# Hybrid decoder layer: an earlier copy of q's sums, other PSUM banks for the woven projections, a larger wait weight

## The chip, the cores and the metric

One core of one Trainium2 chip. The metric is the device time of one execution in microseconds (us). The kernel before takes 595.57 us, the median of three runs (594.65 to 597.58).

## The reference

One decoder layer over 16 meta tokens and 1024 positions, width 1024, everything in float32. An RMS norm is followed by one input projection. Its columns feed two groups of heads that read the same normalised input; the outputs go through one output projection, a residual and a last RMS norm.

```python
u = rmsnorm(h, norm_g)                                  # h: 1040 x 1024
q, k, v, f, z_attn, gate_b, gate_c, xc, z_conv = split(u @ w_in)
cum = cumsum(log_sigmoid(f + b_f))                      # per head
s = q @ k.T / 8 + cum[t] - cum[s]                       # causal, 8 heads x 64
attn = softmax(s) @ v
y_attn = group_rmsnorm(attn, attn_norm_g, 8) * silu(z_attn)
conv = causal_conv3(gate_c * xc, conv_w)                # 512 channels
y_conv = group_rmsnorm(gate_b * conv, conv_norm_g, 8) * silu(z_conv)
out = rmsnorm(h + concat(y_attn, y_conv) @ w_out, final_norm_g)[16:]
```

## The kernel before, in words

Every float32 product is made of three matmuls: each operand is split into a rounded part (`xhi`, `wmhi`, made on ScalarE or GpSimd) and a remainder (`xlo`, `wmlo`, made on VectorE by `lo_vec`, line 115), and hi x hi, hi x lo and lo x hi add up in one PSUM bank.

**First stage, q (lines 179 to 250).** The eight PSUM banks hold the eight sums of q (`psq[m][c]`, four blocks of 128 columns by two halves of the positions): seven tiles of the pool `ps1` and one of `psx`. While inputs arrive, each of eight row slabs adds to all eight banks. After them ScalarE copies the four sums with c = 0 (line 240) and VectorE those with c = 1 (line 241) to SBUF. Ahead of the input projections' scaling stands the row norm: nine loads of `h` through SyncE's queue (line 249), each squared and summed on ScalarE (line 250); `rsqrt_small` (lines 78 to 89) makes the factors, TensorE transposes them into a bank of `psx` (line 259) and VectorE copies them (line 260).

**k, v and the gates (lines 263 to 384).** k's blocks go through the seven `ps1` banks in turn; the first k block takes the bank that q's sum (0, 0) held. Each chunk is scaled by VectorE (`kf`, line 275) and split; q, k and v go to DRAM. The last three chunks of k block 3 take the `ps1` banks 6, 0 and 1, and the `psx` bank last held the transposed decay sums (lines 374 to 377).

**The woven stage (lines 387 to 765).** Here the eight banks are dealt out anew: `pj` (two banks, for the projections), `psn` (three, scores), `pst` (two, transposes), `pso` (one, the products with v). Sixteen half heads of attention are the main work: scores and their exponentials (`s_step`), the end of a softmax (`s_end`: the maximum on VectorE, some small operations on GpSimd, ScalarE and VectorE, then GpSimd scales the exponentials in place, line 635), transposes (`t_step`) and products with v (`v_step`). The twenty projections of the convolution and the gates, in 384 steps of three matmuls, are the filler. `weave` (lines 745 to 760) deals them out: each main step has a cost in us, and after it so many filler steps follow that the rest of the filler is spread evenly over the rest of the main cost; `HEAD` us of filler go ahead of the first scores, `LEFT` us stay. The end of a softmax costs `WAIT`, which stands for no matmul: it draws filler between the scores and the transposes that need the scaled values. `WAIT` has one value for half heads of the one kind, one for the other, and a third for the very first softmax. The filler goes in the order gate c, x, convolution gate, attention gate, gate b for each of four column blocks; with the last step of an x block (line 458) comes a convolution: a scaling pass on GpSimd (line 460) and three passes on VectorE (lines 461 to 463).

TensorE keeps this written order for everything from the first woven projection on. The order of the other engines' instructions, and that of SyncE's DMAs apart from those that are kept in program order, is set by a planner at build time; it may differ from the order of the code.

**Output (lines 769 to 861).** Six of the banks are dealt out again, weights and gated outputs are split as they arrive, and the output projection, residual and last norm follow.

Of the kernel before, what the change touches and what calls it, by code (L numbers as in the profile page):

```python
# [11 lines left out]
AF = mybir.ActivationFunctionType  # L12
ALU = mybir.AluOpType
AX = mybir.AxisListType
PSUM = bass.MemoryType.PSUM
# [20 lines left out]
def hybrid_kernel(ctx, tc, hT, h, w_q, w_vf, w_m, w_o, gn, bf, cw, ga, gc, gf, out):  # L36
    nc = tc.nc
    R_SIDE = "right"
    TABLES = "natural_log_exp_and_others"

    def f(ap):
        return ap.bitcast(F32)
# [49 lines left out]
    def behind(ins):  # L92

        tc.keep_in_program_order(ins)
# [5 lines left out]
    def after(ins, name):  # L100

        tc.add_manual_dep(ins.ins, name, mybir.DependencyInfo(
            mybir.DependencyClass.NoSync, mybir.DependencyReason.SCHED_ONLY), reason="pace")
# [10 lines left out]
    def lo_vec(lo, src, hi):  # L114
        nc.vector.tensor_tensor(lo, src, f(hi), ALU.subtract)  # L115
# [15 lines left out]
    def load_w(m):  # L131
        staged[m] = wp.tile([P, KT, P], F32, name="wm", bufs=1)
        ins = nc.sync.dma_start(staged[m], w_m[m].rearrange("p (k c) -> p k c", k=KT))
        if m < 4:
            behind(ins)

    def split_w(m):
        ws = staged.pop(m)
        whi = wp.tile([P, KT, P], F32R, name="wmhi")
        wlo = wp.tile([P, KT, P], F32R, name="wmlo")  # L140
        hi_pool(whi, ws)
        lo_vec(wlo, ws, whi)
        ready[m] = whi, wlo
# [35 lines left out]
    with ExitStack() as ca:  # L179
# [23 lines left out]
        for i in range(8):  # L203
# [3 lines left out]
        psq = [[(psx if (m, c) == (3, 1) else ps1).tile([P, 512], F32, name="px" if (m, c) == (3, 1) else "ps")  # L207
                for c in range(2)] for m in range(4)]
        with ExitStack() as c1:
            wq = c1.enter_context(tc.tile_pool(name="wq", bufs=3))  # L210
            for k in range(KT):
                ws = wq.tile([P, 512], F32, name="ws")
                xs = wq.tile([P, L], F32, name="xs")
                whi = wq.tile([P, 512], F32R, name="wqhi")
                wlo = wq.tile([P, 512], F32R, name="wqlo")
                if k == 0:
                    behind(nc.sync.dma_start(xs[:, :528], hT[:, 0, :528]))
                behind(nc.sync.dma_start(ws, w_q[k * P:(k + 1) * P, :]))
                (nc.vector.tensor_copy if k == 0 else nc.scalar.copy)(whi, ws)
                for a, b in ((0, 528), (528, L)) if k == 0 else ((0, L),):  # L220
                    if a or k:
                        behind(nc.sync.dma_start(xs[:, a:b], hT[:, k, a:b]))
                    nc.scalar.activation(xhi[k][:, a:b], xs[:, a:b], AF.Copy, scale=gnt[:, k:k + 1])
                    nc.vector.scalar_tensor_tensor(xlo[k][:, a:b], xs[:, a:b], gnt[:, k:k + 1], f(xhi[k][:, a:b]),
                                                   ALU.mult, ALU.subtract)
                lo_vec(wlo, ws, whi)
                todo = [(m, n, c) for m in range(4) for n in range(3) for c in range(2)]
                if k == 0:
                    todo.sort(key=lambda t: t[1:])
                for m, n, c in todo:  # L230
                    wt, xt = ((whi, xhi[k]), (whi, xlo[k]), (wlo, xhi[k]))[n]
                    nc.tensor.matmul(psq[m][c], wt[:, m * P:(m + 1) * P], xt[:, NM + 512 * c:NM + 512 * c + 512],
                                     start=(k == 0 and n == 0), stop=(k == KT - 1 and n == 2))
            load_w(0)
            split_w(0)
            for t, v in ((bft, bf.broadcast_to([P, HEADS])), (cwt, cw), (gat, ga), (gct, gc)):
                behind(nc.sync.dma_start(t, v))
            qraw = [[qk.tile([P, 512], F32, name=f"qraw{m}{c}") for c in range(2)] for m in range(4)]
            for m in range(4):
                nc.scalar.copy(qraw[m][0], psq[m][0])  # L240
                nc.vector.tensor_copy(qraw[m][1], psq[m][1])


            ss = sm.tile([P, 9], F32, name="ss")
            nc.vector.memset(ss, 1.0)
            for j in range(9):
                n = P if j < 8 else NM
                ht = st.tile([P, D], F32, name="ht")
                behind(nc.sync.dma_start(ht[:n], h[j * P:j * P + n, :]))
                nc.scalar.activation(ht[:n], ht[:n], AF.Square, accum_out=ss[:n, j:j + 1])  # L250
        nc.vector.tensor_scalar(ss, ss, 1.0 / D, EPS, ALU.mult, ALU.add)
        rsqrt_small(sm, ss, rtok, "x")
        for b in range(3):
            pr = psx.tile([P, 512], F32, name="px")
            w = 512 if b < 2 else NM
            for i in range(4 if b < 2 else 1):
                j = 4 * b + i
                n = P if j < 8 else NM
# [57 lines left out]
        for j in (0, 1, 2, 3, 5, 6, 7, 4, 8):  # L316
            n = P if j < 8 else NM
# [68 lines left out]

    own = ctx.enter_context(tc.tile_pool(name="own", bufs=1, reuse_waits="tile"))
    cp = ExitStack()
    pj = ctx.enter_context(tc.tile_pool(name="pj", bufs=2, space=PSUM, reuse_waits="tile"))
    psn = cp.enter_context(tc.tile_pool(name="psn", bufs=3, space=PSUM, reuse_waits="tile"))  # L390
    pst = cp.enter_context(tc.tile_pool(name="pst", bufs=2, space=PSUM, reuse_waits="tile"))
    pso = cp.enter_context(tc.tile_pool(name="pso", bufs=1, space=PSUM, reuse_waits="tile"))
# [165 lines left out]
    T_AT = (0.065, 0.08)  # L558
    V_END = 0.975
    V_LAG = 3  # L560
    WAIT = (0, 0.375, 3.3)
    SOON = 0.2
    HEAD = 15.75
    LEFT = 2.75
# [51 lines left out]
    def s_end(c):  # L616

        mx = pnp.tile([P, 4], F32, name="mx")
        nc.vector.tensor_reduce(mx, nmx[c], AX.X, ALU.min)
        e = pnp.tile([P, 4, 3], F32, name="e")  # L620
        nc.gpsimd.tensor_tensor(e, mx.unsqueeze(2).broadcast_to([P, 4, 3]), nmx[c], ALU.subtract)
        nc.scalar.activation(e, e, AF.Exp)
        t = pnp.tile([P, 4, 3], F32, name="t")
        nc.gpsimd.tensor_mul(t, e, smx[c])
        s = pnp.tile([P, 4], F32, name="s")
        nc.gpsimd.tensor_add(s, t[:, :, 0], t[:, :, 1])
        nc.gpsimd.tensor_add(s, s, t[:, :, 2])
        nc.vector.reciprocal(s, s)
        fc = pnp.tile([P, 4, 3], F32, name="fc", bufs=2)
        nc.gpsimd.tensor_mul(fc, e, s.unsqueeze(2).broadcast_to([P, 4, 3]))  # L630
        for i in range(3):
            for j in range(4 * c, 4 * c + 4):
                if i < len(SCH[j]):
                    k0, w = SCH[j][i]
                    nc.gpsimd.tensor_scalar(pn[j][:, k0:k0 + w], pn[j][:, k0:k0 + w], fc[:, j % 4, i:i + 1], 1.0,  # L635
                                            ALU.mult, ALU.mult)
# [70 lines left out]
    def spread(steps, todo, lo, hi):  # L707

        whole = sum(x for x, _ in todo) or 1.0
        at = 0.0  # L710
        for x, s in todo:
            steps.append((lo + (hi - lo) * (at + x / 2) / whole, x, s))
            at += x

    stages = []
    for g in range(-1, 2 * HEADS):
# [3 lines left out]
        if g + 1 < 2 * HEADS:  # L720
# [4 lines left out]
            spread(steps, todo, lo, hi)  # L725
            steps.append((hi, WAIT[g % 2 if g >= 0 else 2], lambda c=c: s_end(c)))
        if g >= 0:
# [55 lines left out]
    def out_mm(n, es):  # L783
        t, c0, w = cells[n]
        tt, cs = slice(t * P, t * P + P), slice(c0, c0 + w)
        for e in es:
            for i, (a, b) in enumerate(((mhi[e], whi[e]), (mhi[e], wlo[e]), (mlo[e], whi[e]))):
                ins = nc.tensor.matmul(held[n][:, :w], a[:, tt], b[:, cs], start=(e == ORDER[0] and i == 0),  # L788
                                       stop=(e == ORDER[-1] and i == 2))
                if n < AHEAD:  # L790
                    pinned(ins)
        return ins.ins.name
# [42 lines left out]
    for i, e in enumerate(ORDER):  # L835
# [7 lines left out]
        for k, n in enumerate(ring):  # L843
            name = out_mm(n, [e])
# [63 lines left out]
```

## Time and profile before

| what | value |
|---|---|
| median of three runs | 595.57 us (594.65 to 597.58) |
| the profiled execution | 596.83 us |
| its span, first to last instruction | 595.1 us |
| TensorE busy, mean granted clock | 578.0 us (97%), 0.995 of full speed |
| VectorE busy | 377.9 us (64%) |
| ScalarE busy | 285.4 us (48%) |
| GpSimd busy | 168.0 us (28%) |

PE is TensorE's matmuls, DVE VectorE, ACT ScalarE, POOL GpSimd, SP the queue of DMA issues on SyncE. Times in the timeline are microseconds from the start of the span. "out<-in" names the tiles that an instruction writes and reads. A bracket at the end of a row is idle time of that engine just before it and what ended it.

### The profile page before, as it was taken

How to read it: one execution, taken by the hardware profiler on the slowest of the kernel's cores; microseconds unless marked ns; L12 is line 12 of the kernel's file. 1: busy time of each engine (PE TensorE's matmuls, PEld its weight loads, DVE VectorE, ACT ScalarE, POOL GpSimd, SP SyncE). 2: the span in 40 equal slices, each digit the busy share in tenths (PEclk: the TensorE clock that was granted, in tenths of full speed). 3: DMA queues.
4: the chain of work that ended last, by engine and by line, in shares of the span. 5: the costliest groups of instructions: out<-in, count | busy, mean ns of one | idle time of the engine just before them, and what ended most of it. 6: DMA issues, size and time to landing. Idle time of an engine off the chain costs nothing.

```text
span 595.1 us, 9156 instructions
## 1 busy us (share of the span) xinstructions
PE 578.0 (97%) x3230; PEld 509.6 (86%) x3230; DVE 377.9 (64%) x834; ACT 285.4 (48%) x667; POOL 168.0 (28%) x290
## 2 busy tenths in 40 slices
PE   9999999999998999999999999999999999899995
PEld 6888999999997889988879997889998887688884
DVE  5415851133367686879776888868869777947432
ACT  5355431131044575556764655747636676705221
POOL 1002010121027244151243254430552416710000
PEclk9999999999999999999999999999999999899999
DMA  8764594249811605415126134251350227453201
GB/s 287 237 194 141 195 341 142 70 147 280 262 39 36 144 35 135 120 57 155 44 75 143 71 108 112 75 143 37 111 197 16 73 88 243 171 205 113 100 35 70
DMA packets 35221, 78.14 MB, mean 131 GB/s; under 512 B 4024, under 2 KB 13384, under 8 KB 35176
## 3 DMA queue, kind: packets, MB, share of 16 engines
q1 hardware_dynamic: 35032, 77.57, 41.6%
q8 instruction: 25, 0.41, 0.3%
q14 instruction: 20, 0.16, 0.1%
q10 hardware_dynamic: 144, 0.00, 0.0%
HBM read 55.92 MB, written 21.64 MB: 130 GB/s over the span
## 4 chain that ended last, share of the span: by engine, by line
PE 71%; DMA 10%; DVE 6%; POOL 4%; ACT 3%; issue 3%; SPq 2%; POOLq 0%; ACTq 0%; DVEq 0%
PE pj L165 30%; PE ps L324 8%; PE p L788 8%; PE pt L645 5%; PE po L669 5%; PE pj L788 4%; PE ps L165 4%; DMA k<-kd 3%; DMA ht<-in_h 3%; PE pn L605 3%; PE pn L606 3%; DMA xs<-in_hT 2%; DVE mlo L115 2%; POOL pn L635 1%; DMA wm<-in_w_m 1%
## 5 line engine op out<-in xcount | busy, mean ns | idle before, releaser
L165 PE MATMUL pj<-xhi,wmhi 128*128 128x512 f32 (+1 forms) x384 | 144.9, 377 | 1.0 <-DVE kf L275 0.5
L165 PE MATMUL pj<-xhi,wmlo 128*128 128x512 f32 (+1 forms) x384 | 137.1, 357 | 0.0
L165 PE MATMUL pj<-xlo,wmhi 128*128 128x512 f32 (+1 forms) x384 | 136.8, 356 | 0.0
L613 ACT ACTIVATE pn<-pn,nmx 128x328 f32<-128x328 f32 (+6 forms) x112 | 60.5, 541 | 52.7 <-DVE nmx L612 27.9
L165 PEld LDWEIGHTS pj<-xhi,wmlo 128*128 128x128 f32 x384 | 72.2, 188 | 8.4
L165 PEld LDWEIGHTS pj<-xhi,wmhi 128*128 128x128 f32 x384 | 72.6, 189 | 6.2 <-issue 1.4
L165 PEld LDWEIGHTS pj<-xlo,wmhi 128*128 128x128 f32 x384 | 72.8, 190 | 3.8
L654 ACT CAST ph<-pt 128x512 fp32r<-128x512 f32 (+4 forms) x112 | 49.6, 445 | 51.0 <-PE po L669 23.3
L635 POOL TENSOR_SCALAR pn<-pn,fc 128x328 f32<-128x328 f32 (+4 forms) x112 | 69.3, 639 | 1.6
L115 DVE TENSOR_TENSOR pl<-pt,ph 128x512 fp32r<-128x512 f32 (+1 forms) x96 | 54.6, 572 | 20.2 <-ACT ph L654 19.5
L112 POOL TENSOR_SCALAR wmhi<-wm 128x1024 fp32r<-128x1024 f32 x24 | 26.2, 1093 | 141.2 <-DMA wm<-in_w_m 81.8
L645 PE MATMUL pt<-ident,pn 128*128 128x128 f32 x288 | 47.4, 273 | 3.9 <-POOL pn L635 2.2
L645 PEld LDWEIGHTS pt<-ident,pn 128*128 128x128 f32 x288 | 36.3, 140 | 14.4 <-POOL pn L635 3.6
L115 DVE TENSOR_TENSOR wmlo<-wm,wmhi 128x1024 fp32r<-128x1024 f32 x24 | 29.4, 1223 | 18.0 <-POOL wmhi L112 17.9
L609 DVE CUSTOM_DVE_ANT_0 pn<-pn,maskn 128x328 f32<-128x328 f32 (+3 forms) x64 | 31.9, 500 | 11.0 <-PE pn L606 9.3
L669 PE MATMUL po<-ph,v 128*128 128x512 f32 (+4 forms) x112 | 37.0, 336 | 0.0
L605 PE MATMUL pn<-k,q 128*128 128x328 f32 (+6 forms) x112 | 36.6, 328 | 0.1
L606 PE MATMUL pn<-k,q 66*128 66x328 f32 (+6 forms) x112 | 36.1, 322 | 0.0
L669 PE MATMUL po<-pl,v 128*128 128x512 f32 (+1 forms) x96 | 33.2, 350 | 0.0
L788 PE MATMUL p<-whi,mlo 128*128 128x512 f32 (+1 forms) x77 | 30.2, 392 | 2.4 <-DVE mlo L115 2.4
L165 PE MATMUL ps<-xhi,wmhi 128*128 128x346 f32 (+1 forms) x96 | 31.0, 323 | 1.1 <-ACT qraw L240 1.1
L612 DVE TENSOR_REDUCE nmx<-pn 128x1 f32<-128x346 f32 (+4 forms) x48 | 24.8, 521 | 9.6 <-PE pn L606 9.6
(227 smaller groups left out, 1229.5 us busy)
## 6 DMA issues: line engine op xcount, KB each, us to landing
wm<-in_w_m SPq DMA_DIRECT2D x24, 512.0 KB, 3.8
k<-kd SPq DMA_DIRECT2D x24, 260.0 KB, 5.3
q<-qd SPq DMA_DIRECT2D x24, 256.0 KB, 5.9
vd<-vv SPq DMA_DIRECT2D x9, 512.0 KB, 2.9
v<-vd SPq DMA_DIRECT2D x8, 576.0 KB, 6.5
ht<-in_h SPq DMA_DIRECT2D x8, 512.0 KB, 5.6
yd<-gy SPq DMA_DIRECT2D x16, 256.0 KB, 2.8
q<-in_w_o SPq DMA_DIRECT2D x8, 512.0 KB, 4.5
```

The source lines that it names most:

```text
L115: nc.vector.tensor_tensor(lo, src, f(hi), ALU.subtract)
L165: ins = nc.tensor.matmul(ps[:, :w], wt[:, k, :], xt[:, t0:t0 + w], start=(k == 0 and n == 0), stop=(k == KT - 1 and n == 2))
L324: nc.tensor.matmul(ps[c][:P if n == P else 48, :260], x[k][:, ts_] if n == P else x[:, k, :], w[k][:, 260 * c:260 * c + 260], start=(k == ...
L605: pinned(nc.tensor.matmul(ps[:, :w], q1[:, qs], k1[:, ks], start=True, stop=False))
L606: pinned(nc.tensor.matmul(ps[:, :w], q2[:DH + 2, qs], k2[:DH + 2, ks], start=False, stop=True))
L609: nc.vector.tensor_tensor_reduce(ps[:, :w], ps[:, :w], maskn[:, MASKW - w:], op0=ALU.add, op1=ALU.min, scale=-1.0, scalar=-NEG, accum_out= ...
L613: nc.scalar.activation(pn[j][:, ks], ps[:, :w], AF.Exp, bias=nmx[c][at], scale=-1.0 if last else 1.0, accum_out=smx[c][at])
L635: nc.gpsimd.tensor_scalar(pn[j][:, k0:k0 + w], pn[j][:, k0:k0 + w], fc[:, j % 4, i:i + 1], 1.0, ALU.mult, ALU.mult)
L645: pinned(nc.tensor.transpose(pt[:, q0:q0 + P], pn[j][:, ks], ident))
L654: nc.scalar.copy(ph[:, at:], pt[:, at:])
L669: pinned(nc.tensor.matmul(po[:, at:], v2[:, vk, :], t[:, at:], start=(kt == 0 and i == 0), stop=(kt == 4 * c + 4 and i == len(parts) - 1)))
L788: ins = nc.tensor.matmul(held[n][:, :w], a[:, tt], b[:, cs], start=(e == ORDER[0] and i == 0), stop=(e == ORDER[-1] and i == 2))
```

## The change

The first copy of q's sums gets a name, and the square of the eighth load (j = 7) is put behind it in ScalarE's order, without a semaphore; the other copies may stand where the planner puts them. The projections' two PSUM banks are taken from the right end of the eight, so that the pools opened after them start at bank 0. The third value of `WAIT` goes from 3.3 to 5.2.

```diff
-                nc.scalar.copy(qraw[m][0], psq[m][0])
+                first = nc.scalar.copy(qraw[m][0], psq[m][0])
                 nc.vector.tensor_copy(qraw[m][1], psq[m][1])
+                if m == 0:
+                    first_out = first.ins.name
...
-                nc.scalar.activation(ht[:n], ht[:n], AF.Square, accum_out=ss[:n, j:j + 1])
+                sq = nc.scalar.activation(ht[:n], ht[:n], AF.Square, accum_out=ss[:n, j:j + 1])
+                if j == 7:
+                    after(sq, first_out)
...
-    pj = ctx.enter_context(tc.tile_pool(name="pj", bufs=2, space=PSUM, reuse_waits="tile"))
+    pj = ctx.enter_context(tc.tile_pool(name="pj", bufs=2, space=PSUM, side=R_SIDE, reuse_waits="tile"))
...
-    WAIT = (0, 0.375, 3.3)
+    WAIT = (0, 0.375, 5.2)
```

## Rows read from the trace of the kernel before

**Rows 1.** The page: busy us, share of the span and instructions of each engine.

```profile
PE 578.0 (97%) x3230; PEld 509.6 (86%) x3230; DVE 377.9 (64%) x834; ACT 285.4 (48%) x667; POOL 168.0 (28%) x290
```

**Rows 2.** PE's waits: engine line <- waited for: us in total, times, longest us.

```profile
PE p L788 <- DVE mlo L115: 2.4, 2, 2.1
PE pt L645 <- POOL pn L635: 2.2, 2, 1.5
```

**Rows 3.** Timeline at the end of q: start, us, engine, line, operation, out<-in, count.

```profile
45.35 0.63 PE L232 MATMUL ps<-xhi,wqlo 128*128 128x512 f32 x2
47.72 1.06 ACT L250 ACTIVATE ht<-ht 128x1024 f32<-128x1024 f32 x1 [2.00 <-DMA ht<-in_h]
49.78 0.40 PE L232 MATMUL px<-xhi,wqlo 128*128 128x512 f32 x1
50.61 2.03 ACT L240 COPY qraw<-ps 128x512 f32<-128x512 f32 x4
51.32 0.40 PE L165 MATMUL ps<-xhi,wmhi 128*128 128x348 f32 x1 [1.14 <-ACT qraw L240]
53.11 0.68 DVE L241 COPY qraw<-px 128x512 f32<-128x512 f32 x1
55.36 0.60 PE L259 MATMUL px<-ident,rtok 128*128 128x128 f32 x4
```

**Rows 4.** Timeline ahead of the first woven projection.

```profile
142.49 0.28 DVE L377 COPY ct<-px 72x128 f32<-72x128 f32 x1
...
147.86 1.23 DVE L115 TENSOR_TENSOR wmlo<-wm,wmhi 128x1024 fp32r<-128x1024 f32 x1 [4.03 <-POOL wmhi L112]
149.66 0.40 PE L165 MATMUL pj<-xhi,wmhi 128*128 128x342 f32 x1 [0.54 <-DVE kf L275]
```

**Rows 5.** Stretch 150 to 160 (engines, PEclk, DMA share, GB/s), then timeline after it.

```profile
150.00:160.00 10.00, 10.00 (x66) 10.00 (x65) 2.27 (x5) 0.52 (x2) 1.05 (x1) 1.00 1.00 301
159.72 1.23 DVE L115 TENSOR_TENSOR wmlo<-wm,wmhi 128x1024 fp32r<-128x1024 f32 x1 [5.47 <-POOL wmhi L112]
161.51 0.40 PE L165 MATMUL pj<-xhi,wmhi 128*128 128x342 f32 x1 [0.30 <-DVE cx L451]
```

**Rows 6.** First softmax: L626 over all heads, its timeline, then chain behind the transposes.

```profile
L626 POOL TENSOR_TENSOR s<-t x16: 197/198/1232, 180.4 to 474.5; 128x4 f32<-128x4 f32 x16
...
176.80 2.18 POOL L460 TENSOR_SCALAR cv<-cx,cwt 128x1024 f32<-128x1024 f32 x1
177.99 0.15 DVE L619 TENSOR_REDUCE mx<-nmx 128x4 f32<-128x12 f32 x1
183.45 5.45 POOL L635 TENSOR_SCALAR pn<-pn,fc 128x328 f32<-128x328 f32 x9
185.76 0.66 PE L645 MATMUL pt<-ident,pn 128*128 128x128 f32 x4 [1.51 <-POOL pn L635]
...
187.56 1.39 PE pj L165 x6
```

**Rows 7.** Timeline of stage two, softmax of head 2 and after.

```profile
257.72 0.16 DVE L619 TENSOR_REDUCE mx<-nmx 128x4 f32<-128x12 f32 x1
260.28 5.03 POOL L635 TENSOR_SCALAR pn<-pn,fc 128x328 f32<-128x328 f32 x9
263.35 0.60 PE L645 MATMUL pt<-ident,pn 128*128 128x128 f32 x4
266.31 1.56 POOL L460 TENSOR_SCALAR cv<-cx,cwt 128x1024 f32<-128x1024 f32 x1
267.63 0.63 PE L645 MATMUL pt<-ident,pn 128*128 128x128 f32 x4 [0.78 <-DVE pl L115]
```

**Rows 8.** Timeline of the softmax with a convolution pass just ahead.

```profile
355.10 1.12 POOL L460 TENSOR_SCALAR cv<-cx,cwt 128x1024 f32<-128x1024 f32 x1
356.13 0.15 DVE L619 TENSOR_REDUCE mx<-nmx 128x4 f32<-128x12 f32 x1
360.33 3.31 POOL L635 TENSOR_SCALAR pn<-pn,fc 128x144 f32<-128x144 f32 x5
```

## The prediction

> **What bounds the kernel now.** Read the page's busy shares first: TensorE (PE) is busy 97% of the span [rows 1], so only its idle time and its order can give anything. The table of PE's waits comes second; its two longest entries are rows 2: the output projection on VectorE (DVE) and the transposes on GpSimd (POOL). Third, the timeline of PE shows three single waits at the places that the diff touches: 1.14 us before the first k block [rows 3], 0.54 us before the first woven projection [rows 4] and 1.51 us before the first transposes [rows 6]. They add up to 3.19 us, 0.53% of the span. Everything else on PE is work that the change leaves alone in amount, so a gain much above that has no source.
>
> The profiled execution took 596.83 us with a span of 595.1, 1.26 us above the median of 595.57. I work out a difference on its timeline and subtract it from the median.
>
> **Part one, the copy ahead of the last square.** The first k block needs the PSUM bank of q's sum (0,0). Its matmuls had been issued by 45.6 us [rows 3], but ScalarE (ACT) copies it out only at 50.61, behind all squares and the small rsqrt, and PE starts at 51.32, 1.14 us after its last q matmul had ended at 50.18. ACT is idle before the square at 47.72 [rows 3], waiting for a load. A copy is a quarter of 2.03 us, 0.51 us, and fits in there, so the square, its load and the statistics behind it stay where they are: this costs nothing as long as the copy is ready before that load lands. On SP nothing is passed: the copy issues no DMA, and no load waits for the seventh square before the small weights behind it. Gain: a q matmul takes 0.40 us and two in a row 0.63 [rows 3], so the next is issued 0.23 us after the last; the k block could start at 50.18 - 0.40 + 0.23 = 50.01 instead of 51.32, **-1.30 us**; ends from 0 (something else is late) to -1.30. What is late next: the transposes of the norms at 55.36 move to 54.06 and need the last q bank, which DVE empties at 53.11 + 0.68 = 53.79. That leaves 0.27 us.
>
> **Part two, the projections' banks.** The two banks from the left belonged to the last two chunks of k block 3. PE waits 0.54 us for DVE to read the first of them, and DVE does that late because it stands in order behind the weight split of line 115, which ran from 147.86 to 149.09 [rows 4]. From the right side the two banks are those of the transposed decay sums, read by 142.77 [rows 4], and of k block 3's first chunk, read just ahead of that. The scores now get the late banks, but 15.75 us of projections stand ahead of them. So this wait goes. The next one of its kind doesn't: at 159.72 DVE again runs such a split, the evacuation of the second projection chunk is behind it, and PE waits until 161.51 [rows 5]. That split waits for weights which come through DMA queues that are full from 150 to 160 (share 1.00) [rows 5]. PE arriving earlier doesn't move them; it only waits longer. I take **0**; the ends are -0.84 (both waits vanish because the evacuation is put ahead of the split) and +0.2, one score bank late.
>
> **Part three, the larger wait weight.** It removes and adds no instruction; it moves projection steps. The scores, transposes and products have a cost of 103.75 in the weave, the projections 204.96, of which 15.75 go ahead and 2.75 stay, so each unit of main cost draws 186.46 / 103.75 = 1.80 of projection; with 1.9 more it is 186.46 / 105.65 = 1.76. At the first end of scores 5.2 instead of 3.3 draws five more steps of 0.64, then they are paid back one by one by all later stages. A 512-wide step takes 0.70 us of PE (six matmuls in 1.39 us [rows 6]), so PE reaches the first transposes 3.5 us of work later. POOL's scaling is ready at 185.7, 1.51 us after PE asked. The wait is covered with 2 us to spare: **-1.51 us**.
>
> Payback costs something, at three places that I found by counting the steps through the loops. First, stage two of the softmax. The last step of block x1 is the 146th; the end of scores came after 139 steps and now comes after 145. So the convolution of x1 starts one step behind the end of scores, not seven. Now POOL gets its scale pass at 266.31, well after the softmax scaling of 260.28 [rows 7]; afterwards it meets the small softmax operations. What that costs is bounded by three chains from the reduced maximum to the start of scaling: 2.56 us undisturbed (257.72 to 260.28) [rows 7], 4.20 us where a convolution pass came just ahead (356.13 to 360.33) [rows 8], 5.46 us in the first stage, with a pass at 176.80 (177.99 to 183.45) [rows 6]. The first four scaling passes take some 2.3 us, so the sums are ready at about 262.6 and PE comes at 263.35: 0.8 us of slack. I take the 4.20, since there the pass also just precedes the maximum: 1.64 - 0.8 = +0.8, and give back half of the 0.78 us wait at 267.63 [rows 7], which falls beside the present place of that pass: **+0.4**. Ends: -0.8 (that wait goes, the chain stays short) and +4.3 (the first stage's 2.9 longer chain, with a 2.18 us pass in front [rows 6], less the slack). Second and third, the transposes of heads 4 and 5 have one projection step less ahead of them, up to 0.70 us each; heads 6 and 7 get one more, where nothing waits now. I take **+0.6**, ends 0 and 1.4.
>
> [...] The row first: the sum of line 626 takes 1.23 us in the first stage, beside the convolution on DVE, and 0.20 us as a median of 16 [rows 6]. [...]
>
> **Sum:** -1.30 + 0 - 1.51 + 0.4 + 0.6 = **-1.8 us**: 595.57 - 1.8 = **593.8 us** (the profiled execution would go from 596.83 to 595.0). 0.5%, about what a measurement of this kernel can tell from no change, is 2.98 us: faster means below 592.6, slower above 598.5.
>
> **Rivals.**
> - *Clean gain*, chance 0.26. The evacuation passes the split (-0.84 for part two), stage two keeps its chain, heads 4 and 5 have enough cover: -1.30 - 0.84 - 1.51 + 0.3 = -3.35, so 592.2. For: nothing on PE's path needs the passed work earlier. Against: DVE's order is set by a planner that put the split first twice [rows 4, 5].
> - *The convolution stops the softmax of stage two*, slower, chance 0.14. Place: between the score end and the first transposes of head 2. Price: up to +4.3, with +1.2 from heads 4 and 5, against -2.81: +2.7, so 598.3, and more if the 0.70 us steps drawn out of later stages uncover further waits for POOL. It decides from 2.8 us of wait at that place. For: the first stage shows the whole price. Against: there the pass preceded the end of scores by one step, here it follows by one.
> - *Part one doesn't deliver*, chance 0.14. The planner puts more copies ahead of the last squares, the norms and their transposes come later, and PE, which runs in order, stands at them by the time it had won. Then only -1.51 + 1.0 = -0.5 is left: 595.1. For: 0.27 us of margin. Against: ACT has 2.0 us idle before that square.
>
> **How the numbers follow.** The forecast has the remaining 0.46; its own range is 592.6 to 595.0. The range 591.6 to 597.0 takes in the clean gain with 0.6 us below it and the payback up to +1.4; left out is most of the slower rival. Faster by over 0.5%: most of the clean case and a little of the forecast, 0.26. Slower: the slower rival where it goes beyond its price, 0.08. The same: 0.66.
>
> **What would show it.** Right: PE's wait for the q copy gone, with the copy near 46 us; no wait at the first woven projection but one of about 1 us at the second projection block; no wait for POOL at the first transposes, with PE there about 2 us later than POOL; a chain of about 4 us from maximum to scaling in stage two. Wrong: PE idle before the k block or at the transposes of the norms; the idle time at the second block shrinking too; waits of over 2 us for POOL at head 2; an output projection that waits on DVE by much more or less than 2.4 us [rows 2], since its start is only carried along here.

## The result, and the profile after

The changed kernel takes 601.48 us, the median of six runs (599.75 to 604.27); beside them the kernel before took 595.11 (593.98 to 597.58). The ratio is 1.0106 [1.0074, 1.0138]: **slower by 1.1%**, where 593.8 and no measurable difference were forecast. The profiled execution took 604.27 us with a span of 602.5. Four executions among all those told of below, two of them of the kernel before, ran at a fraction of the speed (1151, 1464, 1994 and 2014 us) and are left out of the comparisons.

The page's busy line and the table of TensorE's waits, against [rows 1] and [rows 2]:

```profile
PE 581.9 (97%) x3230; PEld 511.4 (85%) x3230; DVE 374.8 (62%) x834; ACT 285.3 (47%) x667; POOL 170.4 (28%) x290
```
```profile
PE po L673 <- DVE ph L115: 3.1, 3, 2.5
PE pt L649 <- DVE pl L115: 2.1, 2, 1.3
PE pt L649 <- POOL pn L639: 1.4, 3, 0.8
PE pj L165 <- DVE cx L455: 1.4, 1, 1.4
...
PE p L792 <- DVE mlo L115: 0.6, 1, 0.6
```

Two things stand out. The longest wait, 2.5 us, is of a kind that was not in the table before: a product (`po`) that waits for a remainder (`ph`, line 115) of VectorE. And the same number of matmuls is busy for 3.9 us more than before (581.9 against 578.0): some of them ran longer.

The timeline of PE shows what became of the single waits. There is none ahead of the k block (50.57) and none at the first transposes (189.32). But the first projections wait, and the third transposes do:

```profile
50.57 0.32 PE L165 MATMUL ps<-xhi,wmhi 128*128 128x348 f32 x1
...
149.38 0.42 PE L165 MATMUL pj<-xhi,wmhi 128*128 128x342 f32 x1 [0.83 <-POOL wmhi L112]
...
163.26 0.40 PE L165 MATMUL pj<-xhi,wmhi 128*128 128x342 f32 x1 [1.35 <-DVE cx L455]
...
189.32 0.60 PE L649 MATMUL pt<-ident,pn 128*128 128x128 f32 x4
...
194.15 0.63 PE L649 MATMUL pt<-ident,pn 128*128 128x128 f32 x4 [1.33 <-DVE pl L115]
...
270.06 0.40 PE L673 MATMUL po<-ph,v 128*128 128x32 f32 x1 [2.53 <-DVE ph L115]
```

To see where time was lost I compare the moments at which TensorE has done the same number of matmul columns in two traces (good to half a us, since some five steps stand elsewhere; the places are times of the kernel before). The changed kernel is 0.8 us ahead at 55 us, 1.8 behind at 165, 0.4 ahead at 190 (the wait of 1.51 [rows 6] is gone), 1.3 behind at 195, 2.5 at 250, 7.5 at 270, 11.6 at 495, and 7.6 from 525 on. The 2.6 us around 150 belong to this execution, in which the weights came late (POOL rounds them at 148.28, after 11.89 us of waiting for the load; before at 146.78): the run of the wait weight alone (e3, below), whose TensorE order is the same, loses 0.3 there, and e4, which has all three parts, 0.4. The largest step is **stage two of the softmax, 250 to 270: 5.0 us**. DVE and POOL there, against [rows 7]:

```profile
263.04 0.17 DVE L623 TENSOR_REDUCE mx<-nmx 128x4 f32<-128x12 f32 x1
...
264.74 1.91 DVE L115 TENSOR_TENSOR wmlo<-wm,wmhi 128x1024 fp32r<-128x1024 f32 x1
266.61 0.34 DVE L115 TENSOR_TENSOR pl<-pt,ph 128x160 fp32r<-128x160 f32 x1
...
266.88 1.26 DVE L465 SCALAR_TENSOR_TENSOR cv<-cx,cwt,cv 128x1024 f32<-128x1024 f32 x1
...
268.53 1.25 DVE L466 SCALAR_TENSOR_TENSOR cv<-cx,cwt,cv 128x1024 f32<-128x1024 f32 x1
269.81 0.19 DVE L115 TENSOR_TENSOR ph<-pt,ph 32x32 fp32r<-32x32 f32 x1
```
```profile
263.25 1.04 POOL L112 TENSOR_SCALAR wmhi<-wm 128x1024 fp32r<-128x1024 f32 x1 [18.16 <-PE pj L165]
264.26 0.21 POOL L625 TENSOR_TENSOR e<-mx,nmx 128x12 f32<-128x12 f32 x1
264.45 1.12 POOL L464 TENSOR_SCALAR cv<-cx,cwt 128x1024 f32<-128x1024 f32 x1
265.54 1.18 POOL L628 TENSOR_TENSOR t<-e,smx 128x12 f32<-128x12 f32 x1
...
267.07 1.13 POOL L631 TENSOR_TENSOR s<-s,t 128x4 f32<-128x4 f32 x1
268.69 1.16 POOL L634 TENSOR_TENSOR fc<-e,s 128x12 f32<-128x12 f32 x1 [0.49 <-DVE s L632]
269.95 2.07 POOL L639 TENSOR_SCALAR pn<-pn,fc 128x328 f32<-128x328 f32 x2
```

In the kernel before the same remainder is done at once, and the weight rounding of line 112 stands behind the softmax scaling:

```profile
259.99 0.19 DVE L115 TENSOR_TENSOR ph<-pt,ph 32x32 fp32r<-32x32 f32 x1
...
265.27 1.05 POOL L112 TENSOR_SCALAR wmhi<-wm 128x1024 fp32r<-128x1024 f32 x1
```

Now that rounding and x1's scale pass (line 464) run inside the softmax chain. Three of its small steps on POOL, some 0.2 us each before, take 1.13 to 1.18 us, and each ends just after a pass of DVE does: 266.72 (the split, 266.65), 268.20 (line 465, 268.14) and 269.85 (line 466, 269.78). From the maximum to the first scaling it is now 6.91 us (263.04 to 269.95) instead of 2.56 [rows 7]. Yet TensorE's wait ends on something smaller: `ph` at 269.81, a 32x32 remainder of 0.19 us that head 1's last product needs. Ahead of it in DVE's order stand a weight split of 1.91 us and two convolution passes, which could start as soon as POOL's rounding and scale pass were there.

The windows (start:end, us, busy time of PE, PEld, DVE, ACT, POOL, then granted clock, DMA share, GB/s) show the second half of the price:

```profile
262.00:268.00 6.00, 5.53 (x31) 4.71 (x28) 5.86 (x14) 1.36 (x6) 4.59 (x6) 1.00 0.16 54
268.00:270.00 2.00, 0.00 (x0) 0.00 (x0) 1.91 (x5) 0.18 (x1) 1.41 (x3) 0.87 0.61 231
270.00:273.00 3.00, 2.94 (x9) 2.58 (x10) 2.76 (x6) 1.33 (x4) 3.00 (x4) 0.50 0.47 127
273.00:277.00 4.00, 4.00 (x16) 3.23 (x15) 1.66 (x4) 2.24 (x6) 2.94 (x6) 0.58 0.14 54
277.00:281.00 4.00, 4.00 (x23) 3.35 (x23) 2.47 (x5) 3.02 (x7) 0.00 (x0) 1.00 0.02 4
```

After 2.53 us without a matmul the granted clock is 0.50 in 270 to 273, and the mean is still 0.58 in 273 to 277. The 512-wide matmuls at 272.60, 273.02 and 273.45 start 0.42 to 0.43 us apart, those at 277.67, 277.90 and 278.13 0.23. An estimate from the granted shares: 3.0 us of 0.50 and 4.0 of 0.58 lose 1.5 + 1.7 = 3.2 us of matmul time. With the 2.53 us of the wait that is 5.7, less the 0.78 us that the kernel before waited in this stage [rows 7]: 4.9, about the step found above.

### The profile page after: what moved, and what is told of

It is laid out like the page before. It is cut to its first block, busy times and chain, and to the rows that moved or that the text cites. A ratio compares the mean times of both kernels' runs of the same rounds, so it can differ in the third digit from the quotient of the medians.

```text
span 602.5 us, 9148 instructions
## 1 busy us (share of the span) xinstructions
PE 581.9 (97%) x3230; PEld 511.4 (85%) x3230; DVE 374.8 (62%) x834; ACT 285.3 (47%) x667; POOL 170.4 (28%) x290
## 4 chain that ended last, share of the span: by engine, by line
PE 51%; DVE 9%; POOL 4%; issue 2%; ACT 2%; POOLq 0%; DVEq 0%; ACTq 0%
PE pj L165 23%; PE p L792 10%; PE pj L792 5%; PE pt L649 5%; PE po L673 4%; PE pn L609 2%; PE pn L610 2%; POOL pn L639 2%; DVE pl L115 1%; POOL wmhi L112 1%; DVE wmlo L115 1%; DVE pn L613 1%; DVE nmx L616 1%; DVE cv L465 1%; DVE cv L466 1%
## 5 line engine op out<-in xcount | busy, mean ns | idle before, releaser
L165 PE MATMUL ps<-xhi,wmlo 128*128 128x346 f32 (+1 forms) x96 | 30.9, 325 | 0.0
```

Of the source, the lines that this page charges most:

```text
L165: ins = nc.tensor.matmul(ps[:, :w], wt[:, k, :], xt[:, t0:t0 + w], start=(k == 0 and n == 0), stop=(k == KT - 1 and n == 2))
```

## The experiments

All are edits of the kernel before or of the changed kernel; each ratio is to runs of the kernel before on the same chip.

**Each part alone.** `e1_copy`, `e2_banks` and `e3_wait`, in this order:

```diff
+                if j == 7:
+                    after(sq, first_out)
...
-    pj = ctx.enter_context(tc.tile_pool(name="pj", bufs=2, space=PSUM, reuse_waits="tile"))
+    pj = ctx.enter_context(tc.tile_pool(name="pj", bufs=2, space=PSUM, side=R_SIDE, reuse_waits="tile"))
...
-    WAIT = (0, 0.375, 3.3)
+    WAIT = (0, 0.375, 5.2)
```

> Part one alone: the first copy of q's sums ahead of the eighth square, all else as before. If the loss is in the softmax of head 2 (theory A), this alone gains: PE's 1.14 us ahead of the first k block goes, about 594.0 against 595.1 before, unless the stretch with full DMA queues (130 to 160 us) takes it back, then 595.1. If the early stages lose (theory B: PE arrives earlier at weights that come later), it is slower, 596 to 597.

> Part two alone: the projections' two banks from the right end; every engine's order of instructions is the one of before. Theory A: no difference that can be measured, 595.1 within 0.5; the 0.54 us wait for VectorE ahead of the first projection goes and comes back at the second block. Theory B: slower by 1 to 3 us, lost between 145 and 165 us.

> Part three alone: the third wait weight at 5.2. Theory A: it holds the whole loss, about 602 (the changed kernel's 601.5 without the gain of the copy), with PE idle by 2 to 3 us near 270 us and the lower clock behind it. Theory B: 598 to 599, the rest belongs to the other parts.

| run | median, us | ratio [95%] |
|---|---|---|
| e1_copy | 595.76 | 1.000 [0.9986, 1.0014] |
| e2_banks | 595.65 | 1.0013 [0.9996, 1.0031] |
| e3_wait | 601.14 | 1.0099 [1.0078, 1.012] |

The wait weight holds the whole loss; the other parts are worth nothing that can be measured. In e2's profile the 0.54 us wait is gone and the one at the second projection block has grown from 0.30 to 1.22:

```profile
160.46 0.40 PE L165 MATMUL pj<-xhi,wmhi 128*128 128x342 f32 x1 [1.22 <-DVE cx L451]
```

In e3's profile the product waits 2.54 us for the same remainder, and the clock falls behind it (0.50 in 268 to 270):

```profile
266.92 0.28 PE L669 MATMUL po<-ph,v 128*128 128x32 f32 x1 [2.54 <-DVE ph L115]
```

**Was there a wait for the copy at all?** e2 and e3 don't have part one, and yet their profiles have no wait ahead of the k block. So the kernel before was profiled again, unchanged:

> The kernel before, unchanged, for a second profile. Theory C (the 1.14 us that TensorE waited ahead of the first k block belonged to the one execution shown: the loads of h landed late in it): the first copy of q's sums is at 48.5 to 49, the k block starts 0.24 us after the last q matmul, and there is nothing for part one to remove. Rival (the wait is the kernel's own and only the banks or the wait weight took it away in the runs so far): the copy is at 50.6 again and the wait over 1 us.

596.13 us, and the copies and the k block were at

```profile
49.28 2.03 ACT L240 COPY qraw<-ps 128x512 f32<-128x512 f32 x4
```
```profile
49.99 0.40 PE L165 MATMUL ps<-xhi,wmhi 128*128 128x348 f32 x1
```

No wait. Of the eight profiles whose copies stand in the old order (before, e2, e3, e5 and, below, e6 to e8 and e10) three have one: 1.14, 1.48 and 0.38 us, 0.38 on average over the eight. The two with over 1 us are those in which the last square of 128 rows starts at 47.72 [rows 3] and 47.92 (e6), waiting for its load; in e5 and e7 it starts at 46.45 and 45.69. The load's landing differed from execution to execution, and the wait with it.

Nor does the new order free the copy from the loads. The planner put the ninth square, of 16 rows, ahead of the copy, and that one waits for a load too. In e12 (below) it waits so long that PE stands ahead of the k block with part one in place; the profile names a memset of GpSimd, which the matmul doesn't read; the copy ended at 51.67, 0.14 us ahead of the matmul:

```profile
50.05 1.06 ACT L252 ACTIVATE ht<-ht 16x1024 f32<-16x1024 f32 x1 [3.08 <-DMA ht<-in_h]
51.11 0.56 ACT L240 COPY qraw<-ps 128x512 f32<-128x512 f32 x1
51.81 0.40 PE L165 MATMUL ps<-xhi,wmhi 128*128 128x348 f32 x1 [1.05 <-POOL ht L315]
```

**One pass put elsewhere.** The changed kernel, with x1's scale pass behind the last scaling pass of head 2's first softmax in POOL's order. TensorE's order is the same.

```diff
-                nc.gpsimd.tensor_scalar(cv, cx[:, 2:1026], cwt[:, i, 2:3], 1.0, ALU.mult, ALU.mult)
+                first = nc.gpsimd.tensor_scalar(cv, cx[:, 2:1026], cwt[:, i, 2:3], 1.0, ALU.mult, ALU.mult)
+                if i in HELD:
+                    after(first, scaled[-1])
```

Here `HELD` is `(1,)`, and `scaled` takes the name of each softmax's last scaling pass.

> The changed kernel, with one thing more: the scaling pass of the second convolution (x1) is put behind the last scaling pass of head 2's first softmax in GpSimd's order. Theory A (the convolution gets into that softmax): the idle time near 270 us and the slow clock behind it go, and with them about 4 to 5 us: 596.5 to 597.5. Theory C (fewer projection steps in all later stages cost the time): less than 1.5 us comes back, 600 to 601.5.

597.6 us, 1.004 [1.0024, 1.0056]: some 3.9 us of the loss come back. The chain from the maximum (260.08) to the scaling (264.23) is 4.15 us, TensorE has no wait of over 0.3 us between 248 and 282, and the clock stays:

```profile
266.00:268.00 2.00, 2.00 (x13) 1.63 (x12) 0.93 (x3) 1.75 (x6) 2.00 (x4) 1.00 0.85 217
268.00:270.00 2.00, 2.00 (x13) 1.76 (x12) 1.86 (x4) 1.12 (x3) 2.00 (x4) 1.00 0.20 82
270.00:273.00 3.00, 3.00 (x20) 2.50 (x19) 3.00 (x7) 2.89 (x7) 0.89 (x1) 1.00 0.02 5
```

The weight rounding (260.31) and the split (261.80, 1.22 us) still fall into the softmax: they lengthen its chain, but without x1's passes beside them no stall comes of it.

**The steps drawn, but paid back at once.** The same weight ahead of the first transposes, and the nine products of the same half head draw as much less. Counted in the trace, six steps more stand there (five in e3), and from head 1 on TensorE's order is that of the kernel before but for a single step at three places.

```diff
-    WAIT = (0, 0.375, 3.3)
+    WAIT = (0, 0.375, 5.2)
+    PAID = 1.9
...
+            if g == 0:
+                back = [n - len(tv) for n, (x, _) in enumerate(tv) if _ in products]
+                for n in back:
+                    at, x, step = steps[n]
+                    steps[n] = (at, x - PAID / len(back), step)
```

> The kernel before with the third wait weight at 5.2, and the 1.9 us of drawn projection work given back at once: the nine products of the same half head draw 1.9 us less, so that from head 1 on TensorE's order is that of the kernel before. Theory A (the loss lies where the payback falls: x1's convolution in head 2's softmax, and fewer steps in later stages): no stall at 270 us, the 1.5 us wait at the first transposes gone, the wait of about 1.3 us for the transposes' remainder just behind them (191 to 194 us) stays; 594.5 to 595.5. Rival B (drawing five more steps ahead of the first transposes costs by itself, in the weights' and banks' order there): 597 or more, with the lag built up before 200 us.

`e7_pay43` has 4.3 and 1.0 in these places (three more steps instead of five), `e8_wait42` only the line `WAIT = (0, 0.375, 4.2)`, so that three more steps are paid back over all later stages.

> The same with a weight of 4.3 and 1.0 us given back: three more steps ahead of the first transposes, the order of the kernel before from head 1 on. Theory A: the wait of 1.5 us for GpSimd goes wholly or down to 0.3, the remainder behind the first transposes is not yet late; 594.0 to 594.6. Rival B: about 596.5, half of the way to 597 or more.

> The kernel before with the third wait weight at 4.2 and nothing else: three more steps ahead of the first transposes, and x1's last step four steps behind the end of head 2's softmax scores' start of its stage count (in the changed kernel one, before seven). Theory A (only the last step's place against head 2's softmax decides): the convolution's passes come early enough for the remainder of head 1's last product to be ready, no stall at 270 us and no clock dip; 594 to 596.5. Rival D (each step moved costs alike wherever the payback falls): half the loss of 5.2, 598 to 599.

| run | median, us | ratio [95%] |
|---|---|---|
| e6_pay52 | 595.14 | 0.9987 [0.9968, 1.0005] |
| e7_pay43 | 594.19 | 0.9981 [0.9961, 1.0001] |
| e8_wait42 | 602.86 | 1.0119 [1.0097, 1.014] |

e6 against e3 (601.14) differs in where the steps are taken back, and in the one step more: that is 6 us. In e7 PE doesn't wait at the first transposes nor just behind them. e8 fell out as neither theory had it: three steps cost more than five. With 4.2 the last step of x1 comes four steps behind the end of scores (seven before, one with 5.2), and now the scaling itself is late. POOL, PE and the clock:

```profile
259.53 1.13 POOL L460 TENSOR_SCALAR cv<-cx,cwt 128x1024 f32<-128x1024 f32 x1
261.90 1.15 POOL L630 TENSOR_TENSOR fc<-e,s 128x12 f32<-128x12 f32 x1 [1.24 <-DVE s L628]
263.15 5.22 POOL L635 TENSOR_SCALAR pn<-pn,fc 128x328 f32<-128x328 f32 x5
```
```profile
266.43 0.66 PE L645 MATMUL pt<-ident,pn 128*128 128x128 f32 x4 [3.79 <-POOL pn L635]
```
```profile
268.00:270.00 2.00, 2.00 (x8) 1.71 (x7) 1.34 (x3) 0.59 (x1) 2.00 (x4) 0.50 0.00 0
270.00:273.00 3.00, 3.00 (x17) 2.53 (x16) 1.00 (x3) 0.97 (x3) 0.62 (x2) 0.80 0.00 0
```

This is the slower rival of the prediction as it was written, at a distance of four steps. The same kernel with x1's scale pass held back as in e4:

> The kernel with a third wait weight of 4.2 (602.86 us, with a stall of 3.8 us for GpSimd's scaling at 266 us), and x1's scale pass put behind the last scaling pass of head 2's first softmax. Theory A (that one pass and the three behind it on VectorE make the stall, and the granted clock that fell to 0.50 behind it makes it larger): the stall and the fall go, 3.8 us and about 1.5 to 2 us for the clock, so 597 to 597.5. Rival F (the stall comes from projection work that arrives ahead of the scaling, whatever GpSimd does): it stays above 601.

598.34 us, 1.0034 [1.001, 1.0058]. Five scaling passes start at 261.36 instead of 263.15 and take 2.78 us instead of 5.22, the 3.79 us wait is 1.13, and the granted clock is 1.00 in every window from 255 to 277:

```profile
261.05 0.20 POOL L633 TENSOR_TENSOR fc<-e,s 128x12 f32<-128x12 f32 x1 [1.58 <-DVE s L631]
261.36 2.78 POOL L638 TENSOR_SCALAR pn<-pn,fc 128x328 f32<-128x328 f32 x5
```

**Payback in one later place.** Two kernels took the steps back in head 2's first products, so that from head 3 on the order is the old one.

The first is e4's kernel with the payback of e6, there:

```diff
-            if g == 0:
+            if g == 4:
```

> The changed kernel with x1's pass held back (597.6 us) and the 1.9 us of drawn work given back in full by the nine products of head 2's first half, so that from head 3 on the order is that of the kernel before. Theory T (what is left of the loss comes from the later stages, which have fewer steps between a softmax and its transposes): 595.5 to 596. Rival U (it comes from heads 0 to 2: the wait for the transposes' remainder at 193 us and the idle 0.7 us between 240 and 255): 597 to 597.6.

603.33 us, 1.0116 [1.0081, 1.0151]. The order that was to hold the pass back named the softmax before, since x1's last step now came ahead of head 2's; the pass ran at 261.88, in front of the chain. Three waits of about 1 us, all of head 1's products for DVE's remainders between convolution passes, and a clock of 0.50 from 270 to 275. This is a test after all: by equal columns it is 0.3 us behind at 250, 7.7 at 285 and 7.7 at the end. One stage made the whole loss, and the later stages in their old order added none. `e13_held` differs in the place of that pass alone:

```diff
+        zc_steps = block_steps(7 + 4 * i, QCH, psumj, zc_done)
+        if i in DEFER:
+            cost, step = zc_steps[DEFER[i]]
+            zc_steps[DEFER[i]] = (cost, lambda step=step, box=box: (box["conv"](), step()))
```

Here `DEFER` is `{1: 5}` and `box["conv"]` issues the four passes of the convolution, the first of them `after(first, scaled[-1])`.

> The kernel of the run before (603.33 us: weight 5.2, payback at head 2, order of the kernel before from head 3 on) with one difference: x1's scale pass is issued five projection steps later and stands behind the scaling passes of head 2's first softmax; TensorE's order is the same. There it stood ahead of that softmax, since the rule that was to hold it back had named the softmax before. Theory A (that pass and the three passes of VectorE behind it are the whole stall): the three waits of 1 us at 266 to 270 and the clock of 0.50 behind them go, some 7 us: 595.5 to 597. On what is left of the changed kernel's loss, T (it comes from the later stages, which have their old order here): 595.5 to 596; U (from heads 0 to 2): 597 to 597.6. Rival F (the stall comes from TensorE's order there, whatever GpSimd does): above 601.

600.61 us, 1.008 [1.0056, 1.0103]: the waits at 266 to 270 are gone (one of 0.48 is left), the chain is 2.66 us (262.03 to 264.69), the clock is 1.00 until 281. That much is as theory A had it. The time isn't, for a new stall stands where this kernel takes its steps back:

```profile
285.06 0.30 PE L664 MATMUL pt<-ident,pn 128*128 128x128 f32 x1 [2.83 <-DVE pl L115]
```
```profile
280.49 1.21 DVE L115 TENSOR_TENSOR wmlo<-wm,wmhi 128x1024 fp32r<-128x1024 f32 x1
...
283.66 0.18 DVE L646 RECIPROCAL s<-s 128x4 f32<-128x4 f32 x1 [0.84 <-POOL s L645]
283.76 0.66 DVE L442 TENSOR_TENSOR zc<-zc,otmp 128x512 f32<-128x512 f32 x1
284.34 0.95 DVE L115 TENSOR_TENSOR pl<-pt,ph 128x416 fp32r<-128x416 f32 x2
```
```profile
286.00:289.00 3.00, 3.00 (x12) 2.58 (x10) 0.50 (x2) 0.48 (x2) 0.93 (x3) 0.55 0.40 158
```

Again a remainder stands late in DVE's order: behind a weight split, passes of the filler and the softmax's reciprocal, for which DVE waits 0.84 us on POOL. Fewer filler steps on PE cover it, by the order; no run tests that. By equal columns 5.0 us are lost here (250 to 285) and 0.2 in all that follows. So e13 doesn't decide between T and U as it was meant to.

**The version that beats both.** e7's weight and payback, with the copy and the banks of the change.

> The weight of 4.3 with 1.0 us given back at once, together with the earlier copy and the other banks. Theory A: nothing is added to 594.2 in most executions, since the other two parts were worth nothing alone; where an execution's loads of h land late (a wait of 0 to 1.5 us ahead of the k block in the profiles so far) the copy saves that wait: 593.3 to 594.2, and no wait ahead of the k block in its profile. Rival (the copy disturbs the norms or the planner's order): 595 or more.

> The kernel of the weight of 4.3 with 1.0 us given back at once, the earlier copy and the other banks again, for a profile that can be read (the one shown for it took 2013 us). Theory A: 593 to 594.5, no wait ahead of the k block, none for GpSimd at the first transposes, no fall of the clock in stage two. Rival (the gain of 0.4% was of that one chip's runs): 595 or more.

593.63 us, 0.996 [0.9937, 0.9982], and again 594.37, 0.9975 [0.9954, 0.9996]: faster than before by 0.25 to 0.4%. Whether copy and banks add to e7 these runs can't tell (the intervals overlap). In e14's profile neither the k block nor the first transposes wait, and what part two only moves is there, 1.30 us at the second projection block:

```profile
49.85 0.32 PE L165 MATMUL ps<-xhi,wmhi 128*128 128x348 f32 x1
...
160.37 0.40 PE L165 MATMUL pj<-xhi,wmhi 128*128 128x342 f32 x1 [1.30 <-DVE cx L455]
...
185.05 0.60 PE L650 MATMUL pt<-ident,pn 128*128 128x128 f32 x4
```

## Why the prediction was wrong

**Part one, -1.30 us: wrong.** The step that failed is the price read from one execution. The wait is gone in the profiles of e1 and of the changed kernel, but e1 is at 1.000. The copy doesn't stand near 46 us, as forecast, but at 46.93 in e1 and at 48.97 in the changed kernel, behind the square of 16 rows. The 1.14 us [rows 3] depend on when a load lands; in five of eight profiles there was nothing to gain. A mean of 0.38 us is below what these measurements can tell (the interval of e1 is 1.7 us wide). The third rival gave the right size for another reason: nothing was late in e1, whose transposes of the norms start at 54.78 without a wait, 0.58 us before those of [rows 3].

**Part two, 0: right**, with its mechanism. DVE's split waits 5.47 us for POOL's rounding [rows 5], the rounding at 158.63 waits 10.27 us for the weights' load, the queues are full (share 1.00 from 150 to 160 [rows 5]), and PE, when it is earlier, waits longer at the second block (1.22 us in e2, 0.30 before). In the eight profiles with the old banks (before, e1, e3, e5 to e8, e10) the waits at the two places add up to 0.80 to 1.24 us; in e2 it is 1.22, all at the second block.

**Part three at the first transposes, -1.51: right as far as it went.** The wait is gone in e3, e4 and the changed kernel. Missed was the next thing late: PE, no longer stopped there, waits 1.33 us at 194 for a remainder that stands behind a weight split (192.17, 1.23 us). With three steps more instead of five that wait doesn't arise (e7).

**Part three at stage two, +0.4: this is the step that failed.** Place and cause were named: x1's convolution one step behind the end of scores. Three things were wrong. First, the size: I took 4.20 us [rows 8] for the chain from maximum to scaling; it was 6.91, above even the 5.46 of the first stage. I had counted x1's passes alone; the next weights' rounding and split come with the same last step, and in e4, without x1's passes, they make 4.15 of the undisturbed 2.56. Second, the waiting step: only PE's wait for POOL's scaling was priced, and 0.8 us of slack set against it. The stall came earlier on PE, at head 1's last product, whose 0.19 us remainder stood behind 4.4 us of split and convolution on DVE. Third, the stall was counted at its length: the clock that fell behind it (0.50 and 0.58) took 3.2 us, by the estimate above, on top of 2.53. By equal columns the stage (250 to 270) costs 3.6 us in e3 and 5.0 in the changed kernel, where +0.4 stood in the sum; holding back the one pass returned 3.9 us (e4) and 4.5 (e10 against e8), and in e13 it removed the stall of this stage, TensorE's order being the same in each pair. The "for" of the slower rival was the better argument, and its chance of 0.14 as well as the high end of 597.0 were too low.

The row of line 626, 1.23 us in the first stage and 0.20 as a median [rows 6], has its like in the runs: the same `fc` takes 1.15 us in e8, with x1's convolution ahead of the scaling, and 0.20 in e10, where it is held back, and five scaling passes take 5.22 and 2.78. In the changed kernel each of the three long steps on POOL ends 0.06 or 0.07 us after a pass of DVE. Why a step on POOL takes longer there, no run shows.

**Part three in later stages, +0.6: wrong in size, then cancelled.** By equal columns e3 loses 4.1 us from 270 to 495. Its timeline has nine waits of 0.2 to 0.8 us there, together 3.4, most of them for POOL's scaling and DVE's remainders, and two more, together 1.1, at the start of the output projection. The kernel before has three in this stretch, together 1.7. So the waits account for 2.8 of that loss; the rest stays open. e3 wins 4.0 back by 525. There stood the output projection's wait of over 2 us and the lower clock behind it (0.58 in 517 to 520 of the kernel before): a later TensorE finds VectorE done. That the two together, +0.1, come near the +0.6 is luck. I had written that this wait is "only carried along"; in the changed kernel it is 0.6, with a clock of 1.00 from 515 to 530. For the whole of e3 the terms are: first transposes -2.1, behind them +1.7, 195 to 250 +1.2, stage two +3.6, later stages +4.1, output -4.0, together +4.5 against a measured 5.6.

What stays open is how the 2 us that e4 still loses divide. The trace puts +2.4 between 165 and 355, +3.5 in the later stages and -4.0 at the output; no run isolates one of these.

## What to carry to other kernels

When a filler is moved to cover one wait, follow the vector passes that its last steps set free into the stage where they now fall, and read every engine's order there: the step that stalls may be a small one queued behind them, not the one whose cover you counted. Take the moved work back in the same stage if you can; here that was the difference between no loss (e6) and 1% (e3). And price no wait from a single profile: one that hangs on a load's landing needs a second look before anything is built on it.

## What was not expected of the hardware

The price of a stall wasn't linear here. Waits of 1.51 us [rows 6] and 1.13 us (e10) left the granted clock at 1.00. Waits of 2.1 (the output projection before), 2.53, 2.54, 2.83 and 3.79 us were followed by 0.50 to 0.58 in a window within the next 4 us. It wasn't the length of a single wait alone: in e12 the three of 1.03, 1.02 and 0.90 us, which ended at 266.18, 267.67 and 269.63, were followed by 0.50 from 270 to 275. How long it lasted differed for the same wait: after 2.54 us in e3, ended at 266.92, the clock was 0.83 in 270 to 272 and 1.00 from there; after 2.53 us in the changed kernel, ended at 270.06, it was 0.50 in 270 to 273 and 0.58 on average in 273 to 277.
